# Log-sigmoid of the forget gates: one operand of each step in PSUM, the steps issued as one piece on VectorE

## The chip, the core and the metric

The kernel runs on one core of a Trainium2 chip. The metric is the device time of one execution in microseconds, from repeated runs; a profile is one further execution, taken by the hardware profiler. The work of the core is done by five engines that run at the same time, each with its own queue of instructions in a fixed order: TensorE (PE; its weight loads are PEld), VectorE (DVE), ScalarE (ACT), GpSimd (POOL) and SyncE (SP), which issues the transfers.

## What is computed

One layer of a streaming encoder on 512 tokens of 1024 channels, in float32: a half-step feed-forward block, then a mixing block, then a second half-step feed-forward block and a last RMS norm. In the mixing block one projection gives a convolution branch (512 channels, causal depthwise convolution of width 31, layer norm, swish) and an attention branch of 8 heads with 64 channels each. The attention has forget gates, which are what the change is about:

```
log_f = jax.nn.log_sigmoid(f_logit)               # (batch, 512, 8)
cum = jnp.cumsum(log_f, axis=1).transpose(0, 2, 1)
...
s = einsum("bqhd,bkhd->bhqk", qb, kb) * scale
s = s + cum[:, :, q0:q1, None] - cum[:, :, None, :q1]
s = where(kpos <= qpos, s, -inf)
p = softmax(s, axis=-1)
```

So no score of any head can be finished before the log-sigmoids of all tokens are there and summed up along the sequence.

## The kernel before, in words

**Products.** Channels lie on the 128 partitions and tokens along the free axis. Every large product is made in three passes of reduced precision: a weight tile of 128x1024 is loaded (raw), ScalarE makes its high part (whi), VectorE the low part (wlo, line 427), and TensorE multiplies whi with the high and the low part of the activations and wlo with the high part, eight groups of three matmuls of 512 columns for a tile (`product`, line 512). Three raw buffers and two of whi and wlo go round (line 60).

**Order of the mixing block** (line 51): the four convolution tiles c0 to c3, the values and gate logits (v), attention 0 and 1 (two heads each), the convolution branch's norm (n), attention 2 and 3, then the output projection. The convolutions 1 and 3 run on VectorE as 31 scalar_tensor_tensor steps each, with the accumulator in a PSUM bank (line 659); 0 and 2 run as a multiplication on ScalarE (tap) and an addition on GpSimd (acc, lines 664 and 665).

**Gates** (`values`, line 676). The product with the value and gate weights is spread over four banks; zf (128 tokens x 4 groups x 8 heads, so 32 numbers on each partition) is made from them by eight small VectorE steps (line 706). Then comes the log-sigmoid (lines 712 to 725): e1 = min(-z, z), e1 = exp(e1) on ScalarE, y = e1 / (e1 + 2), a series in y squared with nine terms, and lf = min(z, 0) - 2 times the series. All four tiles e1, e2, e3 and lf are in SBUF. For each half of the heads lf is copied to lfs (line 731), TensorE transposes it into a bank pc (line 735), a scan on VectorE gives the running sum (line 738), which goes to DRAM (cumd) and comes back spread over the partitions as ck (line 796) for the softmax of each head (lines 811 to 817). The transposed probabilities go through the bank of tag "pt", of which there is one (line 818).

**What sets the order.** All instructions are first recorded, then a planner in the kernel (`Plan.schedule`, line 245) puts them in an order for each engine, by prices of its own (`price`, line 221) and by ranks, the length of what hangs on an instruction plus an urgency (200 for the log-sigmoid, line 68). At each step it takes the instruction that can start first; of those that can start at the same moment, the one of highest rank. It counts 0.13 us from the end of a VectorE instruction to the start of one that reads its result (line 145), and 0.15 us to one on another engine. Between two `join` calls (line 172) all that is recorded is one unit: it is priced as the sum of its prices and nothing is put between its parts. The large products are kept in the order in which they are recorded (`in_turn`, line 507), a group of three matmuls being a unit; other work of TensorE is put between the groups. On the chip each engine runs its instructions in that fixed order, and waits where an input is late.

Of the kernel before, what the change touches and what calls it, by code (L numbers as in the profile page):

```python
# [24 lines left out]
F32 = mybir.dt.float32  # L25
F32R = mybir.dt.float32r
BF16 = mybir.dt.bfloat16
AF = mybir.ActivationFunctionType
ALU = mybir.AluOpType
AX = mybir.AxisListType  # L30

P = 128
# [9 lines left out]
H = 8  # L42
HD = 64
NT = T // P
# [15 lines left out]
LOADS, SPLITS, MISC, PT = 3, 2, 1, 1  # L60
# [280 lines left out]
def block_kernel(ctx: ExitStack, tc, x_d, w13a, w2a, wag, wvf, wqk, wo, w13b, w2b, par_d, out_d):  # L341
    nc = tc.nc
    plan = Plan(tc)
    V, S, PE = plan.engine("V", nc.vector), plan.engine("S", nc.scalar), plan.engine("PE", nc.tensor)
# [3 lines left out]
    pp = ctx.enter_context(tc.tile_pool(name="pp", bufs=1, space=bass.MemoryType.PSUM))  # L348
    dr = ctx.enter_context(tc.tile_pool(name="dr", bufs=1, space=bass.MemoryType.DRAM))

    def tile_(shape, tag, name, bufs=1, dt=F32):
        return plan.tile(sb, shape, dt, tag, name, bufs)

    def bank(tag, name, bufs=1):
        return plan.tile(pp, [P, T], F32, tag, name, bufs)

    def product_bank(name):
        return bank("mm", name, 3)

    def slot(n, name, dt=F32):  # L360

        return tile_([P, T], f"r{n}", name, 1, dt)
# [37 lines left out]
    for w13, w2 in ((w13a, w2a), (w13b, w2b)):  # L400
# [3 lines left out]
        if w13 is w13a:  # L404
            for piece in ORDER.split():
                n = int(piece[1:] or 0)
# [6 lines left out]
    def unit():  # L413
        i = taken[0]
        taken[0] += 1
        src, idx, k, c = units[i]
        raw = tile_([P, k, c], "raw", f"raw{i}", LOADS)
        hi = tile_([P, k, c], "whi", f"whi{i}", SPLITS, F32R)
        lo = tile_([P, k, c], "wlo", f"wlo{i}", SPLITS, F32R)
        load_and_split(i, raw, hi, lo, 0, k)  # L420
        return hi, lo
# [85 lines left out]
    def in_turn(step):  # L507

        for o in stream:
            step.before[id(o)] = o  # L510
# [162 lines left out]
    zf = tile_([P, NT, H], "zf", "zf")  # L673
    cum = []

    def values():
        plan.urgency = URGENT_V
        pr = bank("misc", "pr", MISC)
        PE.transpose(pr[:, :P], st.compact, ident)
        rcol = tile_([P, NT], "rcol", "rcol")  # L680
        V.tensor_copy(rcol, pr[:, 0:P:32])
        plan.urgency = 0.0
        for c in range(2):
            pv = [product_bank(f"pv{c}_{t}") if t < 2 else bank("s", f"pv{c}_{t}", 2) for t in range(NT)]
            for kh in range(2):
                hi, lo = unit()
                for t in range(NT):
                    ts_ = slice(t * P, (t + 1) * P)
                    o = pv[t][:, :VC]
                    head = None  # L690
                    for k in range(KD // 2):
                        kk = kh * (KD // 2) + k
                        step = plan.join("PE", head)
                        if head is None:
                            head = step
                            in_turn(step)
                        PE.matmul(o, xh[kk][:, ts_], hi[:, k], start=kk == 0, stop=False)
                        PE.matmul(o, xh[kk][:, ts_], lo[:, k], start=False, stop=False)
                        PE.matmul(o, xl[kk][:, ts_], hi[:, k], start=False, stop=kk == KD - 1)
                        plan.join(None)  # L700
                    stream[:] = [step]
            plan.urgency = URGENT_V
            for t in range(NT):
                rc = rcol[:, t:t + 1]
                S.activation(vt[:, t, 4 * HD * c:4 * HD * (c + 1)], pv[t][:, :4 * HD], AF.Copy, scale=rc)
                V.scalar_tensor_tensor(zf[:, t, 4 * c:4 * c + 4], pv[t][:, 4 * HD:VC], rc,
                                       par[:, G_FB + 4 * c:G_FB + 4 * c + 4], ALU.mult, ALU.add)
            plan.urgency = 0.0

        plan.urgency = URGENT_LF  # L710

        lf, e1, e2, e3 = (tile_([P, NT, H], n, n) for n in ("lf", "e1", "e2", "e3"))
        V.tensor_scalar(e1, zf, -1.0, None, ALU.mult)
        V.tensor_tensor(e1, e1, zf, ALU.min)
        S.activation(e1, e1, AF.Exp)
        V.tensor_scalar(e2, e1, 2.0, None, ALU.add)
        V.reciprocal(e2, e2)
        V.tensor_mul(e1, e1, e2)
        V.tensor_mul(e2, e1, e1)
        V.tensor_scalar(e3, e2, 1.0 / 17.0, None, ALU.mult)  # L720
        for n in (15, 13, 11, 9, 7, 5, 3):
            V.scalar_tensor_tensor(e3, e3, 1.0 / n, e2, ALU.add, ALU.mult)
        V.scalar_tensor_tensor(e3, e3, 1.0, e1, ALU.add, ALU.mult)
        V.tensor_scalar(e1, zf, 0.0, None, ALU.min)
        V.scalar_tensor_tensor(lf, e3, -2.0, e1, ALU.mult, ALU.add)


        for g in range(2):
            lfs = tile_([P, NT, P], "ew", f"lfs{g}", BUFS["ew"])
            G.memset(lfs, 0.0)  # L730
            V.tensor_copy(lfs[:, :, 0::32], lf[:, :, 4 * g:4 * g + 4])
            pc = bank("misc", f"pc{g}", MISC)
            plan.join("PE")
            for t in range(NT):
                PE.transpose(pc[:, t * P:(t + 1) * P], lfs[:, t], ident)
            plan.join(None)
            cs = slot((21, 14)[g], f"cum{g}")
            V.tensor_tensor_scan(cs, one, pc, 0.0, ALU.mult, ALU.add)

            rows = plan.tile(dr, [4, T], F32, f"cum{g}", f"cumd{g}")  # L740
            with plan.urgent(500.0):
                Q.dma_start(out=rows, in_=cs[0::32, :])
            cum.append(rows)

        plan.urgency = 0.0
# [134 lines left out]
    for piece in ORDER.split():  # L880
        n = int(piece[1:] or 0)
        if piece[0] == "c":
            conv_tile(n)
        elif piece[0] == "v":
            values()
        elif piece[0] == "a":
            attention(n)
        elif piece[0] == "n":
            plan.urgency = URGENT_LN
            rconv = conv_norm()  # L890
            plan.urgency = 0.0
        else:
            part = n // 2
            if n == 2:
                rattn = attn_stats.rstd()
            for j in range(2):
                w = unit()
                for d in (4 * (n % 2) + 2 * j, 4 * (n % 2) + 2 * j + 1):
                    w_out(part, d, w, rattn if part else rconv)
# [57 lines left out]
```

## Time and profile before

| | us |
|---|---|
| median of 3 runs | 980.85 |
| lowest, highest | 977.52, 983.25 |
| the profiled execution, its time | 982.02 |
| the profiled execution, its span (first to last instruction) | 979.0 |

Times inside the profile count from the start of the span. In a timeline a row gives the start, the duration, the engine, the line (a helper's line, L217, for all of them, so rows are told apart by the tiles), the operation, and out<-in with partitions x elements; behind it, in brackets, the idle time of that engine just before and what ended it. Buffer numbers are left out of the names: e is e1, e2 or e3, and conv the accumulator of convolution 3 in this stretch. A duration includes the time in which an instruction has started and is held up. [...]

### The profile page before, as it was taken

What the parts mean: (1) busy time and instruction counts of PE and PEld (TensorE: products, weight loads), DVE (VectorE), ACT (ScalarE), POOL (GpSimd) and SP (SyncE); (2) the same over time, 40 slices, a digit from 0 to 9 for tenths busy, and PEclk for the clock granted to TensorE, in tenths of its full rate; (3) what the DMA queues carried; (4) which work ended last, traced back from release to release, by engine and by line L of the source; (5) the groups of instructions that cost most, each with busy time, mean ns of one, the idle gap of its engine ahead of it and who ended that gap; (6) DMA issues with size and microseconds to landing.
All of it is one profiled execution on the core that took longest, in us unless ns stands there. A gap on an engine that the chain in (4) does not pass through costs nothing.

```text
span 979.0 us, 11641 instructions
## 1 busy us (share of the span) xinstructions
PE 953.4 (97%) x4687; PEld 777.2 (79%) x4687; DVE 518.5 (53%) x730; ACT 368.3 (38%) x528; POOL 109.8 (11%) x102
## 2 busy tenths in 40 slices
PE   8999999999999999996999999999999999999996
PEld 7888888888888888894666777888888888888885
DVE  6544442244444444989887867444443244444433
ACT  6423221123233325666558655332321122323230
POOL 2000000000000002899432100000000000000000
PEclk9999999999999999999898999999999999999998
DMA  7222332222233222221221212222332222223202
GB/s 242 85 90 104 105 116 88 79 93 101 88 114 118 89 86 74 88 93 71 71 71 34 87 51 80 95 99 89 113 118 90 85 86 89 105 93 132 90 30 87
DMA packets 26838, 91.07 MB, mean 93 GB/s; under 512 B 2840, under 2 KB 6040, under 8 KB 26784
## 3 DMA queue, kind: packets, MB, share of 16 engines
q1 hardware_dynamic: 26784, 90.33, 27.1%
q8 instruction: 36, 0.59, 0.2%
q14 instruction: 18, 0.15, 0.0%
HBM read 88.21 MB, written 2.11 MB: 92 GB/s over the span
## 4 chain that ended last, share of the span: by engine, by line
PE 86%; DVE 6%; ACT 2%; POOL 2%; DMA 1%; issue 1%; SPq 0%; DVEq 0%; POOLq 0%; ACTq 0%
PE f2o L217 12%; PE f2g L217 12%; PE f2u L217 12%; PE f1o L217 12%; PE f1u L217 12%; PE f1g L217 12%; PE wo L217 5%; DVE conv L217 2%; POOL acc L217 2%; PE pg L217 1%; PE pa L217 1%; PE po L217 1%; DVE e L217 1%; DMA x<-x_d 1%; PE s L217 1%
## 5 line engine op out<-in xcount | busy, mean ns | idle before, releaser
L217 ACT CAST whi<-raw 128x1024 fp32r<-128x1024 f32 (+3 forms) x153 | 165.9, 1085 | 476.8 <-issue 223.7
L217 DVE TENSOR_TENSOR wlo<-raw,whi 128x1024 fp32r<-128x1024 f32 (+3 forms) x153 | 198.2, 1296 | 30.8 <-ACT whi L217 29.1
L217 POOL TENSOR_TENSOR acc<-acc,tap 128x512 f32<-128x512 f32 x60 | 88.9, 1482 | 35.0 <-ACT tap L217 30.1
L217 PE MATMUL f2o<-f2ah,whi 128*128 128x512 f32 (+1 forms) x198 | 72.7, 367 | 0.0
L217 PE MATMUL f2o<-f2al,whi 128*128 128x512 f32 (+1 forms) x198 | 72.3, 365 | 0.0
L217 PE MATMUL f2o<-f2ah,wlo 128*128 128x512 f32 (+1 forms) x198 | 72.3, 365 | 0.0
L217 PE MATMUL f1u<-xh,whi 128*128 128x512 f32 x176 | 68.8, 391 | 0.6 <-ACT xh L217 0.6
L217 PE MATMUL f1u<-xl,whi 128*128 128x512 f32 x176 | 68.7, 390 | 0.3 <-DVE xl L217 0.3
L217 PE MATMUL f2g<-xh,whi 128*128 128x512 f32 x176 | 68.7, 390 | 0.0
L217 PE MATMUL f2u<-xh,whi 128*128 128x512 f32 x176 | 68.6, 390 | 0.0
L217 PE MATMUL f1u<-xh,wlo 128*128 128x512 f32 x176 | 68.5, 389 | 0.0
L217 PE MATMUL f2g<-xh,wlo 128*128 128x512 f32 x176 | 68.5, 389 | 0.0
L217 PE MATMUL f2u<-xh,wlo 128*128 128x512 f32 x176 | 68.5, 389 | 0.0
L217 PE MATMUL f2g<-xl,whi 128*128 128x512 f32 x176 | 68.5, 389 | 0.0
L217 PE MATMUL f1o<-f1ah,whi 128*128 128x512 f32 x176 | 68.5, 389 | 0.0
L217 PE MATMUL f1o<-f1al,whi 128*128 128x512 f32 x176 | 68.5, 389 | 0.0
L217 PE MATMUL f1o<-f1ah,wlo 128*128 128x512 f32 x176 | 68.5, 389 | 0.0
L217 PE MATMUL f2u<-xl,whi 128*128 128x512 f32 x176 | 68.5, 389 | 0.0
L217 PE MATMUL f1g<-xh,whi 128*128 128x512 f32 x168 | 65.5, 390 | 0.3 <-ACT whi L217 0.3
L217 PE MATMUL f1g<-xl,whi 128*128 128x512 f32 x168 | 65.5, 390 | 0.0
L217 PE MATMUL f1g<-xh,wlo 128*128 128x512 f32 x168 | 65.5, 390 | 0.0
L217 DVE TENSOR_TENSOR f2un<-f2u,rstd_f2in 128x512 f32<-128x512 f32 x22 | 15.2, 692 | 71.8 <-PE f2u L217 71.8
(231 smaller groups left out, 1768.1 us busy)
## 6 DMA issues: line engine op xcount, KB each, us to landing
raw<-w13b SPq DMA_DIRECT2D x44, 512.0 KB, 3.2
raw<-w13a SPq DMA_DIRECT2D x42, 512.0 KB, 3.3
raw<-w2a SPq DMA_DIRECT2D x16, 704.0 KB, 4.1
raw<-w2b SPq DMA_DIRECT2D x16, 704.0 KB, 4.0
raw<-wag SPq DMA_DIRECT2D x8, 512.0 KB, 3.2
raw<-wqk SPq DMA_DIRECT2D x8, 512.0 KB, 3.2
raw<-wo SPq DMA_DIRECT2D x8, 512.0 KB, 3.2
raw<-wvf SPq DMA_DIRECT2D x4, 520.0 KB, 3.1
```

The source lines that it names most:

```text
L217: ins = getattr(target, method)(*real, **kw)
```

## The change

The negation and the minimum become one instruction. One PSUM tile of tag "pt", with four slices p1 to p4, takes the exponential, the denominator (later min(z, 0)), y and y squared. Each later step reads at most one operand from SBUF and one from PSUM; the quotient is formed twice, once into PSUM (p3) and once into SBUF (e1), to multiply one by the other. The 16 VectorE steps after the exponential are recorded between `plan.join("V")` and `plan.join(None)`.

```diff
--- before.py
+++ after.py
@@ -707,22 +707,27 @@
                                        par[:, G_FB + 4 * c:G_FB + 4 * c + 4], ALU.mult, ALU.add)
             plan.urgency = 0.0
 
+
+
         plan.urgency = URGENT_LF
-
         lf, e1, e2, e3 = (tile_([P, NT, H], n, n) for n in ("lf", "e1", "e2", "e3"))
-        V.tensor_scalar(e1, zf, -1.0, None, ALU.mult)
-        V.tensor_tensor(e1, e1, zf, ALU.min)
-        S.activation(e1, e1, AF.Exp)
-        V.tensor_scalar(e2, e1, 2.0, None, ALU.add)
-        V.reciprocal(e2, e2)
-        V.tensor_mul(e1, e1, e2)
-        V.tensor_mul(e2, e1, e1)
-        V.tensor_scalar(e3, e2, 1.0 / 17.0, None, ALU.mult)
+        ps = plan.tile(pp, [P, 16, NT, H], F32, "pt", "e", PT)
+        p1, p2, p3, p4 = (ps[:, n] for n in range(4))
+        V.scalar_tensor_tensor(e1, zf, -1.0, zf, ALU.mult, ALU.min)
+        S.activation(p1, e1, AF.Exp)
+        plan.join("V")
+        V.tensor_scalar(p2, p1, 2.0, None, ALU.add)
+        V.reciprocal(e2, p2)
+        V.tensor_mul(p3, p1, e2)
+        V.tensor_mul(e1, p1, e2)
+        V.tensor_mul(p4, p3, e1)
+        V.tensor_scalar(e3, p4, 1.0 / 17.0, None, ALU.mult)
         for n in (15, 13, 11, 9, 7, 5, 3):
-            V.scalar_tensor_tensor(e3, e3, 1.0 / n, e2, ALU.add, ALU.mult)
-        V.scalar_tensor_tensor(e3, e3, 1.0, e1, ALU.add, ALU.mult)
-        V.tensor_scalar(e1, zf, 0.0, None, ALU.min)
-        V.scalar_tensor_tensor(lf, e3, -2.0, e1, ALU.mult, ALU.add)
+            V.scalar_tensor_tensor(e3, e3, 1.0 / n, p4, ALU.add, ALU.mult)
+        V.scalar_tensor_tensor(e3, e3, 1.0, p3, ALU.add, ALU.mult)
+        V.tensor_scalar(p2, zf, 0.0, None, ALU.min)
+        V.scalar_tensor_tensor(lf, e3, -2.0, p2, ALU.mult, ALU.add)
+        plan.join(None)
 
 
         for g in range(2):
```

## Rows read from the trace of the kernel before

**Rows 1.** Page, busy time and share of the span of each engine

```profile
PE 953.4 (97%) x4687; PEld 777.2 (79%) x4687; DVE 518.5 (53%) x730; ACT 368.3 (38%) x528; POOL 109.8 (11%) x102
```

**Rows 2.** Stretches: PE, PEld, DVE, ACT, POOL busy (instructions), PEclk, DMA

```profile
442.00:467.00 25.00, 15.59 (x68) 11.59 (x67) 24.91 (x39) 14.21 (x20) 21.45 (x16) 0.89 0.18 63
```

**Rows 3.** Timeline of TensorE, 444 to 467 us

```profile
444.84 0.50 PE L217 MATMUL pk<-xh,wlo 128*128 128x512 f32 x1 [0.70 <-DVE wlo L217]
...
445.89 0.40 PE L217 MATMUL pk<-xh,whi 128*128 128x512 f32 x1
...
451.35 0.50 PE L217 MATMUL pq<-xh,wlo 128*128 128x512 f32 x1 [0.73 <-DVE wlo L217]
...
457.36 0.46 PE L217 MATMUL s<-k,q 128*128 128x128 f32 x2 [0.73 <-DVE k L217]
...
460.51 0.50 PE L217 MATMUL pk<-xh,wlo 128*128 128x512 f32 x1 [1.78 <-DVE wlo L217]
466.46 1.12 PE L217 MATMUL pc<-ident,lfs 128*128 128x128 f32 x4 [5.46 <-DVE lfs L217]
```

**Rows 4.** Timeline of VectorE in the chain's stretch, 442 to 467 us

```profile
442.27 0.17 DVE L217 TENSOR_SCALAR e<-zf 128x32 f32<-128x32 f32 x1
...
443.06 0.59 DVE L217 TENSOR_TENSOR e<-e,zf 128x32 f32<-128x32 f32 x1
443.57 1.21 DVE L217 TENSOR_TENSOR wlo<-raw,whi 128x1024 fp32r<-128x1024 f32 x1
...
455.93 0.68 DVE L217 SCALAR_TENSOR_TENSOR e<-e,e 128x32 f32<-128x32 f32 x1
...
457.13 0.83 DVE L217 SCALAR_TENSOR_TENSOR e<-e,e 128x32 f32<-128x32 f32 x1
...
466.24 0.24 DVE L217 COPY lfs<-lf 128x16 f32<-128x16 f32 x2
```

**Rows 5.** Instructions that read or write the chain's tiles e1 to e3

```profile
L217 DVE SCALAR_TENSOR_TENSOR e<-e,e x8: 614/786/1269, 451.2 to 462.2; 128x32 f32<-128x32 f32 x8
...
L217 DVE RECIPROCAL e<-e x1: 340/340/340, 446.6 to 446.6; 128x32 f32<-128x32 f32 x1
L217 DVE TENSOR_TENSOR e<-e,e x1: 173/173/173, 447.4 to 447.4; 128x32 f32<-128x32 f32 x1
```

**Rows 6.** Timeline of GpSimd, two additions of convolution 2

```profile
455.27 1.30 POOL L217 TENSOR_TENSOR acc<-acc,tap 128x512 f32<-128x512 f32 x1
...
456.64 1.27 POOL L217 TENSOR_TENSOR acc<-acc,tap 128x512 f32<-128x512 f32 x1
```

**Rows 7.** Groups of VectorE instructions in 380 to 560 us

```profile
L217 DVE SCALAR_TENSOR_TENSOR conv<-u,par,conv 128x512 f32<-128x512 f32 x60 | 44.8, 747 | 0.7
```

**Rows 8.** Instructions that write the gate logits zf (duration min/median/max)

```profile
L217 DVE SCALAR_TENSOR_TENSOR zf<-pv,rcol,par x8: 206/216/224, 425.5 to 441.5; 128x4 f32<-128x4 f32 x8
```

**Rows 9.** Timeline of VectorE, an instruction and one that reads its result

```profile
553.09 0.68 DVE L217 TENSOR_TENSOR t<-wo,rstd_conv 128x512 f32<-128x512 f32 x1
553.81 0.69 DVE L217 TENSOR_TENSOR x<-x,t 128x512 f32<-128x512 f32 x1
```

**Rows 10.** Timeline of ScalarE, the chain's exponential

```profile
443.68 0.23 ACT L217 ACTIVATE e<-e 128x32 f32<-128x32 f32 x1 [0.22 <-DVE e L217]
```

**Rows 11.** Busy time in stretches of 5 us, the columns of rows 2

```profile
465.00:470.00 5.00, 3.54 (x11) 2.96 (x12) 4.97 (x8) 0.00 (x0) 0.61 (x1) 0.50 0.01 2
...
490.00:495.00 5.00, 3.22 (x24) 2.24 (x22) 5.00 (x5) 2.82 (x6) 4.13 (x3) 1.00 0.53 170
495.00:500.00 5.00, 4.79 (x24) 3.30 (x25) 4.23 (x16) 2.07 (x7) 0.00 (x0) 0.66 0.01 3
...
530.00:535.00 5.00, 3.10 (x15) 1.73 (x16) 3.57 (x8) 4.99 (x8) 2.94 (x3) 0.80 0.01 3
```

**Rows 12.** Timeline of VectorE, softmax scaling steps of attention 0

```profile
492.12 2.83 DVE L217 TENSOR_SCALAR sm<-sm,st 128x512 f32<-128x512 f32 x2
...
510.48 0.48 DVE L217 TENSOR_SCALAR sm<-sm,st 128x512 f32<-128x512 f32 x1
```

## The prediction

> **What bounds the kernel now.** I read the page first. TensorE is busy for 97% of the span and VectorE for about half [rows 1], so a faster VectorE chain is worth only what TensorE waits for it. Next I read the table of stretches, to find where TensorE is not busy: in 442 to 467 us it is busy for 15.59 of 25 us while VectorE is busy for 24.91 [rows 2]. There, and for these 25 us only, VectorE is the bound. The timeline of TensorE names the waits one by one [rows 3]: 0.70 us and 0.73 us for a low part of a weight (wlo), 0.73 us for k, 1.78 us for the next wlo, and 5.46 us for lfs, the product of the log-sigmoid chain: 9.40 us together. TensorE runs its instructions in order, so while the transposes of lfs wait, the rest of the key product of attention 1 waits behind them.
>
> Then I read VectorE in the same stretch [rows 4]. The chain starts at 442.27 and its result is copied to lfs at 466.24, 24.0 us for 17 small steps on 32 columns and one exponential. Two things make it long. First, the planner puts one other instruction (a convolution tap, a wlo, a piece of q or k) between any two steps. Second, a step itself takes a median of 786 ns in the eight-fold form, while the same size took 173 ns once [rows 5]. What is the difference? The step that starts at 455.93 ends at 456.61 and the one at 457.13 ends at 457.96 [rows 4]; GpSimd's additions of the other convolution end at 456.57 and 457.91 [rows 6]. Steps end when a GpSimd instruction ends. So most of a step is a wait for GpSimd, and the chain goes at GpSimd's pace, one step for each addition, about 1.37 us. The convolution taps in between take SBUF u and a PSUM accumulator, and the mean of sixty is 747 ns for 512 columns [rows 7]: they don't show that wait.
>
> [...]
>
> **The change part by part.** Removed: the separate -z and minimum become one instruction, and the steps after the exponential each read one operand from PSUM. Added: one multiplication more (the quotient is formed twice), so the piece has 16 instructions where 15 stood. Moved: the piece is one unit to the planner. No DMA is added; the loads of cumd and ck move up on SP's queue with the chain, past weight loads that are issued well ahead, at no cost. The PSUM bank is the one of tag "pt", whose first other use is attention 0's transposes, which follow from cum and so cannot come earlier: cost nothing.
>
> What a step costs now is in no row, since no row has 32 columns with PSUM. Bounds: below, the uncontended step of 173 ns [rows 5]; above, the 747 ns of a tap that also reads and writes PSUM [rows 7]. The nearest is zf, 216 ns for 4 columns with a PSUM input [rows 8]. From 4 to 512 columns the time goes from 216 to 747 ns, 1.05 ns a column, so 32 columns give 0.245 us. A dependent step starts a little after the end of the one before: 553.81 after 553.09 + 0.68, 0.04 us [rows 9]. So 15 steps of 0.28 us and a reciprocal of 0.34 + 0.07 us [rows 5] are 4.6 us; by the lower bound it is 16 x 0.21 = 3.4 us, by the upper 16 x 0.79 = 12.6 us. I take 4.6, as zf is of the same kind and size.
>
> [...]
>
> Start of the piece: the first step at 442.27 (0.17), a tap, then wlo, which stood behind the second step at 443.57 and can now start at 443.06; it takes 1.2 [rows 4], to 444.3. The exponential ran at 443.68 [rows 10], and now needs only the first step. By the planner's prices (lines 221 to 243) a tap then goes first, as it is ready a hair sooner. So the piece runs from about 444.9 to 449.5, another tap goes in before the copy (0.7), and the copy, with both sides in SBUF, may wait half of one GpSimd addition: lfs at 450.9.
>
> What waits behind the piece on VectorE? The wlo and q of the next products, by 4.6 us at most; the wlo is wanted by TensorE at 451 (0.73 late before), but TensorE is standing at lfs by then.
>
> Where does TensorE stand? This is the term that decides. The planner orders TensorE by its own prices. Before, it counted 15 steps of 0.10 with one 0.66 tap each, 12.7 with two wlo in place of taps; the piece is priced 6 x 0.095 + 0.265 + 9 x 0.098 = 1.71, plus one tap. So in its own clock (which gives an order here and no time) the chain ends 10.4 sooner, and it moves the transposes up by 15 groups of three matmuls (0.65 each) and two s products: from behind the first group of the second pk to behind the second group of the first pk. TensorE gets there early: its third pk matmul started at 444.84, the seventh at 445.89 [rows 3], both now about 0.5 earlier, 445.4. It waits from 445.4 to 450.9, **5.5 us**: the wait for lfs is not removed, it moves forward. The planner's 1.71 for a piece that takes 4.6 is the reason.
>
> The sum: waits before 9.40; after 5.5 for lfs and 0.2 for the first wlo. The second wlo, the k and the third wlo (0.73, 0.73, 1.78) have VectorE 5 to 6 us less loaded and come in time. Gain 9.40 - 5.7 = 3.7. [...] The profiled execution took 982.02 (span 979.0 and 3.0 around it): 978.3 by this gain. It stands 1.2 above the median of the three runs, 980.85, so the forecast is **977.1**. By the piece's lower bound (1.2 sooner) it is 975.9; with a step of 0.4 us it is 979.
>
> **Rivals.** *More comes back* (0.22). Attention 0 starts some 10 us sooner, and VectorE has slack. TensorE idles 1.78 us in 490 to 495 behind softmax steps and is at 0.66 of its clock in 495 to 500, another 1.7 us [rows 11]. If both go: 977.1 - 3.5 = 973.6; with the piece at its lower bound too, 972.4. For it: VectorE was full there. Against: GpSimd still adds then.
>
> *Given back* (0.12). In 530 to 535 TensorE is busy 3.10 of 5 us and ScalarE 4.99 [rows 11]: the output projection waits for the convolution branch's norm. If that chain doesn't move up, TensorE waits the 3.7 there: 980.9. Against: that chain follows TensorE's own sums.
>
> *The step's price stays* (0.07). If GpSimd is not the cause, or writing PSUM is dear, 16 steps of 0.79 without pause put lfs at 458.4+, waits are 13.2 against 9.4: 984.7. It decides from 0.52 us a step. The change would then shorten nothing.
>
> *Attention 0 meets GpSimd* (0.14), the slower side. Its eight scale-by-1/sum steps, SBUF to SBUF, are moved up among the taps of GpSimd. Two of 512 columns took 2.83 us among taps, one 0.48 when GpSimd was idle [rows 12]: 0.94 lost each, 7.5 for eight. 1.8 of that is in the wait of 490 to 495 already. If the planner's new order makes TensorE stand for the rest, with half speed after two such waits: 977.1 + 5.7 + 3.4 = 986.2. It is slower than before from 3.7 us of such waits on. Against: before, most of them already ran among taps.
>
> **How the numbers follow.** The forecast has 0.45, with a range of its own of 974.5 to 979.5. About 0.5%, 4.9 us, is what a measurement of this kernel can tell. Faster by more (below 975.9): all of the first rival and some 0.4 of the forecast, 0.40. Slower by more (above 985.8): two thirds of the last rival and some of the third, 0.13. The rest 0.47. The range leaves out the tail of the first rival and the last one: 970 to 984.5.
>
> **What would show it.** Right: steps of 0.2 to 0.3 us in one block, about 4.6 us, near 445; lfs near 451; TensorE's wait for lfs of 4 to 6 us inside the first pk, with half clock behind it; no waits for wlo and k over 0.3 us up to 470; 467 to 560 nearly as before. Wrong: steps over 0.5 us; a wait for lfs under 3 us; or TensorE waits on softmax over 4 us before 500.

## The result, and the profile after

The changed kernel takes **969.14 us** (median of 6 runs, 968.43 to 970.01) and the kernel before took 979.06 us beside it (6 runs, 975.9 to 983.25). The ratio is 0.9892 [0.9874, 0.9910]: 9.9 us or 1.1% faster. The forecast of 977.1 had the sign right and the size too small, and the time lies below the range. A later pair on another occasion gave 969.3 and 978.34.

First the page of the changed kernel, the line that answers to [rows 1]. TensorE's busy time falls by 4.1 us although it computes the same: part of the gain is not a shorter wait but a faster clock (a mean of 0.992 in its profiled execution, 0.985 in that of before).

```profile
PE 949.3 (98%) x4687; PEld 774.7 (80%) x4687; DVE 511.9 (53%) x730; ACT 368.3 (38%) x528; POOL 109.8 (11%) x102
```

Next the stretches, with the columns of [rows 2] and [rows 11]; PEclk is the clock granted to TensorE, as a share of its full speed.

```profile
442.00:467.00 25.00, 20.79 (x90) 16.28 (x89) 22.84 (x53) 14.46 (x27) 18.27 (x13) 0.86 0.31 94
...
445.00:450.00 5.00, 0.97 (x6) 0.84 (x5) 4.52 (x20) 3.73 (x5) 4.69 (x5) 0.66 0.28 97
450.00:455.00 5.00, 5.00 (x19) 4.04 (x18) 3.87 (x4) 0.72 (x1) 3.85 (x3) 0.66 0.31 107
...
490.00:495.00 5.00, 4.93 (x28) 2.60 (x27) 4.88 (x14) 2.07 (x7) 1.91 (x1) 1.00 0.30 105
495.00:500.00 5.00, 5.00 (x25) 4.04 (x25) 4.87 (x13) 4.17 (x9) 0.52 (x1) 1.00 0.32 105
...
520.00:525.00 5.00, 3.49 (x21) 1.80 (x20) 4.87 (x10) 4.99 (x8) 2.96 (x3) 1.00 0.02 3
525.00:530.00 5.00, 4.39 (x41) 2.08 (x39) 4.97 (x7) 4.95 (x9) 2.67 (x4) 1.00 0.01 2
530.00:535.00 5.00, 5.00 (x40) 3.95 (x32) 3.16 (x11) 4.61 (x10) 0.00 (x0) 1.00 0.66 207
```

In the chain's own stretch TensorE is busy for 20.79 us where it was for 15.59 [rows 2]. It still stands idle in 445 to 450 and runs at a granted clock of 0.66 there and in the five us behind. In 490 to 500 it no longer stands, and the clock that was 0.66 in 495 to 500 [rows 11] is 1.00. The stretches from 520 on matter as much: TensorE idles 2.1 us between 520 and 530, about as much as it idled before in this part of the kernel, and yet the clock stays at 1.00. The kernel before, in the same view, had this behind its idle time of 530 to 535 [rows 11]:

```profile
535.00:540.00 5.00, 5.00 (x25) 2.40 (x28) 3.66 (x6) 4.12 (x7) 2.70 (x4) 0.52 0.06 15
```

That is nearly five us at half the full clock (0.52), which the prediction had not read. These are TensorE's waits near 495 and 530 in the kernel before:

```profile
495.21 1.02 PE L217 MATMUL s<-k,q 128*128 128x256 f32 x2 [1.99 <-DVE st L217]
...
530.25 0.30 PE L217 MATMUL pt<-ident,sm 128*128 128x128 f32 x1 [0.36 <-DVE sm L217]
531.20 0.73 PE L217 MATMUL s<-k,q 128*128 128x512 f32 x2 [0.66 <-DVE st L217]
...
532.56 0.42 PE L217 MATMUL ssq_conv<-sq_conv,ones 128*32 128x128 f32 x8 [0.55 <-POOL sq_conv L217]
...
534.11 0.79 PE L217 MATMUL wo<-yl,whi 128*128 128x512 f32 x1 [0.44 <-DVE yl L217]
```

Now TensorE's timeline in the changed kernel. Its waits answer to those of [rows 3].

```profile
443.93 0.50 PE L217 MATMUL pk<-xh,wlo 128*128 128x512 f32 x1 [0.18 <-DVE wlo L217]
...
444.73 0.40 PE L217 MATMUL pk<-xh,wlo 128*128 128x512 f32 x1
449.16 1.11 PE L217 MATMUL pc<-ident,lfs 128*128 128x128 f32 x4 [4.03 <-DVE lfs L217]
...
521.54 0.74 PE L217 MATMUL s<-k,q 128*128 128x512 f32 x2 [1.16 <-DVE st L217]
...
524.08 0.50 PE L217 MATMUL wo<-yl,whi 128*128 128x512 f32 x1 [0.35 <-DVE yl L217]
...
526.08 0.44 PE L217 MATMUL pt<-ident,sm 128*128 128x128 f32 x2 [0.22 <-ACT pT L217]
...
527.71 0.50 PE L217 MATMUL wo<-yl,whi 128*128 128x512 f32 x1 [0.38 <-DVE yl L217]
```

The four waits for wlo, wlo, k and wlo [rows 3] are down to one of 0.18 us. The wait for lfs is still there, 4.03 us where it was 5.46, and it has moved forward by 17 us into the first pk. VectorE's timeline of the changed kernel shows why it is so long:

```profile
441.87 0.19 DVE L217 SCALAR_TENSOR_TENSOR e<-zf 128x32 f32<-128x32 f32 x1
...
444.45 0.19 DVE L217 TENSOR_SCALAR e<-e 128x32 f32<-128x32 f32 x1
...
445.99 1.74 DVE L217 SCALAR_TENSOR_TENSOR e<-e,e 128x32 f32<-128x32 f32 x8
...
447.99 0.19 DVE L217 SCALAR_TENSOR_TENSOR lf<-e,e 128x32 f32<-128x32 f32 x1
448.10 0.75 DVE L217 SCALAR_TENSOR_TENSOR conv<-u,par,conv 128x512 f32<-128x512 f32 x1
448.76 0.42 DVE L217 COPY lfs<-lf 128x16 f32<-128x16 f32 x2
```

The piece is one block, its steps starting 0.2 to 0.4 us apart, from 444.45 to 448.18, 3.73 us, beside GpSimd at work for 4.69 of the 5 us. The eight-fold step has this row among the instructions on the tiles e (against [rows 5]):

```profile
L217 DVE SCALAR_TENSOR_TENSOR e<-e,e x8: 186/187/189, 446.0 to 447.5; 128x32 f32<-128x32 f32 x8
```

Where did the time come from? I added up TensorE's idle time in stretches of 1 us, and what its busy time lost to the clock (busy time times one minus the granted clock), from 440 to 560 us. In us, idle / lost to the clock:

| profiled execution | span | 440–480 | 480–515 | 515–560 | span less all of it |
|---|---|---|---|---|---|
| before | 979.0 | 9.43 / 2.55 | 2.10 / 1.65 | 2.02 / 3.19 | 958.1 |
| after | 967.1 | 4.62 / 2.14 | 0.07 / 0 | 2.11 / 0 | 958.2 |

The remainder is the same, so these terms add up to the whole difference of 11.9 us between the spans: 6.7 us of idle time (4.8 in the chain's stretch, 2.0 near 495) and 5.2 us of clock (0.4, 1.65 and 3.2). The medians differ by 9.9 only, since the profiled execution of before (982.02) lies 3 us above the median of its runs.

### The profile page after: what moved, and what is told of

Its sections match the earlier page's. It is cut to its first block, busy times and chain, and to the rows that moved or that the text cites. A ratio compares the mean times of both kernels' runs of the same rounds, so it can differ in the third digit from the quotient of the medians.

```text
span 967.1 us, 11642 instructions
## 1 busy us (share of the span) xinstructions
PE 949.3 (98%) x4687; PEld 774.7 (80%) x4687; DVE 511.9 (53%) x730; ACT 368.3 (38%) x528; POOL 109.8 (11%) x102
## 3 DMA queue, kind: packets, MB, share of 16 engines
HBM read 88.21 MB, written 2.11 MB: 93 GB/s over the span
## 4 chain that ended last, share of the span: by engine, by line
PE 89%; DVE 4%; POOL 3%; ACT 2%; issue 1%; DMA 0%; SPq 0%; DVEq 0%; POOLq 0%; ACTq 0%
PE f2o L217 13%; PE f2g L217 12%; PE f2u L217 12%; PE f1o L217 12%; PE f1g L217 12%; PE f1u L217 12%; PE wo L217 5%; POOL acc L217 3%; PE pk L217 2%; PE pq L217 1%; PE pg L217 1%; PE pa L217 1%; PE po L217 1%; PE s L217 1%; DVE conv L217 1%
```

## The experiments

My theory after the result: the PSUM operands free the steps of GpSimd, the planner's low price for the piece leaves the wait for lfs, and the rest of the gain is the clock near 500 and 535. The rivals: that joining alone is enough; that the gain near 495 and 535 comes from the order only; and that the clock falls independently of the waits.

**The PSUM operands without the joined piece.**

```diff
-        plan.join("V")
...
-        plan.join(None)
```

> The changed kernel without the join: the steps keep their PSUM operand but are recorded one by one, so other VectorE work may stand between them. Lock theory (a step with SBUF operands waits for GpSimd): steps of about 0.19 us with one tap of 0.66 between them, lfs near 457 us, no wait of TensorE for lfs over 1 us, as TensorE gets to the transposes only near 458; 966 to 970 us if the removed waits are all that counts. Order theory (the gain comes from the piece being together): steps of 0.6 to 0.8 us as before, lfs near 465, 979 us. Attention theory (the later gain comes from attention 0 starting earlier): waits gone but half clock at 495 to 500 and 530 to 540 stays, 972 to 975 us.

It took 971.22 us, ratio 0.9913 [0.9883, 0.9944]. Three rows of VectorE's timeline, then the first transposes of lfs on TensorE's, both of this kernel:

```profile
452.58 0.18 DVE L217 SCALAR_TENSOR_TENSOR e<-e,e 128x32 f32<-128x32 f32 x1
452.68 0.75 DVE L217 SCALAR_TENSOR_TENSOR conv<-u,par,conv 128x512 f32<-128x512 f32 x1
453.33 0.18 DVE L217 SCALAR_TENSOR_TENSOR e<-e,e 128x32 f32<-128x32 f32 x1
```

```profile
457.23 0.72 PE L217 MATMUL pc<-ident,lfs 128*128 128x128 f32 x4 [2.09 <-DVE lfs L217]
```

A step takes 0.18 us and the chain still goes, for the most part, at one step for each other instruction, but with a tap between them the next step now starts 0.75 us later (452.58 to 453.33) instead of about 1.37. The wait for lfs is 2.09, shorter than in the changed kernel, because the planner left the transposes late. So the operands alone give 7.6 of the 9.9 us (the two intervals overlap). The lock theory holds for the steps and for lfs near 457, but it missed the wait (under 1 us) and the time (up to 970). In the terms of the table this kernel has 3.77 / 1.67, 0.08 / 0 and 3.35 / 3.04 us: the stretch of 480 to 515 is free as in the changed kernel, but the half clock behind 520 stays, as the attention theory had it for that place. The operands alone do not remove it.

**The joined piece without the PSUM operands**, in the kernel before:

```diff
+        plan.join("V")
         V.tensor_scalar(e2, e1, 2.0, None, ALU.add)
...
         V.scalar_tensor_tensor(lf, e3, -2.0, e1, ALU.mult, ALU.add)
+        plan.join(None)
```

> The kernel before with the steps after the exponential joined into one piece, all operands in SBUF. Lock theory: each of the 15 steps still waits for a GpSimd addition, about 1.3 us each, the piece takes 15 to 20 us, TensorE waits 15 to 20 us for lfs, 985 to 992 us. Order theory: with nothing in between the steps are 0.2 us, the piece takes 4 us, 969 us.

979.04 us, ratio 0.9992 [0.9975, 1.0008]: joining alone is worth nothing. The steps on the tiles e, and TensorE's wait, in this kernel:

```profile
L217 DVE SCALAR_TENSOR_TENSOR e<-e,e x8: 193/665/1302, 448.9 to 454.5; 128x32 f32<-128x32 f32 x8
```

```profile
455.89 1.11 PE L217 MATMUL pc<-ident,lfs 128*128 128x128 f32 x4 [9.72 <-DVE lfs L217]
```

The piece takes 9.6 us (445.50 to 455.08), less than the 15 to 20 that I expected, and the time is below the 985 to 992 that went with it: only seven additions ran beside the 15 steps, and some steps follow another at 0.19 us without meeting one. The 9.72 us at one place took the place of most of the five waits, and the idle time of 440 to 480 even grew (11.97 against 9.43). The wait near 495 is gone here too (0 / 0), which wins that back, and 515 to 560 stays as before (1.80 / 3.22).

**Is it GpSimd?** The same kernel without GpSimd's additions of convolution 2:

```diff
-                G.tensor_add(a, a, t)
+                if i != 2:
+                    G.tensor_add(a, a, t)
```

> The joined piece with all operands in SBUF, as in the run join_only, with the 30 additions of convolution 2 on GpSimd left out, so that convolution 2 is the first tap only. Lock theory: with GpSimd idle the SBUF steps take about 0.19 us each, as the PSUM steps do, and the piece about 3.6 us instead of 9.6, with lfs near 449. Rival (SBUF operands or the piece itself are slow): steps of 0.6 to 1.1 us stay and the piece takes 9 us or more.

One execution, of 969.21 us; it leaves out a part of the layer, so only the steps are compared. A row of the tiles e:

```profile
L217 DVE SCALAR_TENSOR_TENSOR e<-e,e x8: 191/192/194, 446.2 to 447.8; 128x32 f32<-128x32 f32 x8
```

With both inputs in SBUF and GpSimd's additions gone, a step is 192 ns and the piece 3.5 us (444.94 to 448.42). Nothing of the instructions themselves was slow: the 665 ns are GpSimd's doing. That is shown.

**The planner's price for the piece.** It priced the piece at 1.71 where it takes 3.73. Two prices of my own: the number is added to the planner's, so that the piece counts 3.7, about what it takes, and then 6.2, more than it takes:

```diff
-        plan.join("V")
+        plan.join("V").cost = 2.0
```

> The changed kernel with 2.0 us added to the planner's price of the piece, which then is 3.7, what the piece takes on the chip. The transposes move behind the sixth group of the first pk. Theory that the wait for lfs is the planner's under-pricing: the wait falls from 4.0 to 1 to 1.5 us, the half clock behind it goes or shortens, 964 to 967 us. Rival (what is won there is given back later, since another order follows): the wait falls and the time stays at 968 to 970.

```diff
-        plan.join("V")
+        plan.join("V").cost = 4.5
```

> The changed kernel with 4.5 us added to the planner's price of the piece. The transposes move behind the first group of the second pq, attention 0 starts some 5 us later than in the changed kernel in the planner's order. Theory of the under-pricing: no wait for lfs, no half clock near 450, 963 to 966 us. Attention theory: the later start brings the half clock at 495 to 540 back, 967 to 972 us.

The first took 976.05 us (0.9966 [0.9946, 0.9987]), the second 969.41 (0.9893 [0.9861, 0.9926]). With 2.0, VectorE and TensorE show:

```profile
448.91 2.09 DVE L217 TENSOR_TENSOR wlo<-raw,whi 128x1024 fp32r<-128x1024 f32 x1
450.93 1.31 DVE L217 COPY lfs<-lf 128x16 f32<-128x16 f32 x2
```

```profile
452.22 1.12 PE L217 MATMUL pc<-ident,lfs 128*128 128x128 f32 x4 [3.51 <-DVE lfs L217]
...
528.70 0.65 PE L217 MATMUL ssq_conv<-sq_conv,ones 128*32 128x128 f32 x8 [4.00 <-POOL sq_conv L217]
```

Both expectations are missed. The wait hardly fell (3.51, where I expected 1 to 1.5), as a wlo went ahead of the two copies to lfs, which are SBUF to SBUF and took 1.31 us beside GpSimd's additions instead of 0.42 (0.25 in the kernel without the additions). A new order also put a wait of 4.00 us before the sums of the convolution branch. A small change of price moved the time by 7 us, most of it far from the chain. With 4.5, TensorE shows:

```profile
451.37 0.66 PE L217 MATMUL pc<-ident,lfs 128*128 128x128 f32 x4 [0.67 <-DVE lfs L217]
...
519.68 0.30 PE L217 MATMUL pt<-ident,sm 128*128 128x128 f32 x1 [0.81 <-DVE sm L217]
...
520.65 0.43 PE L217 MATMUL ssq_conv<-sq_conv,ones 128*32 128x128 f32 x8 [0.67 <-POOL sq_conv L217]
...
522.20 0.80 PE L217 MATMUL wo<-yl,whi 128*128 128x512 f32 x1 [0.70 <-DVE yl L217]
```

Here the wait for lfs is as good as gone and the clock does not fall behind it: 3.47 / 0 in 440 to 480 against 4.62 / 2.14, which is 3.3 us better. Of these only 1.15 are idle time, as other waits come in, 0.62 us for a wlo and 1.02 for q among them. So the price decides where this wait lies and how long it is, but the price that is right for the piece, 2.0 more, did not remove it. The time is that of the changed kernel: three waits of 0.81, 0.67 and 0.70 us within 3 us are followed by half clock, which costs 3.27 us in 515 to 560. In the profiled execution the gain is given back there. The four runs of this kernel fall into two groups, 967.7 and 968.5 us at a mean clock of 0.995, and 970.3 and 970.9 at 0.992.

**The copies inside the piece**, to take the tap and the wlo from between the chain and lfs:

```diff
+        lfss = [tile_([P, NT, P], "ew", f"lfs{g}", BUFS["ew"]) for g in range(2)]
+        for lfs in lfss:
+            G.memset(lfs, 0.0)
         plan.join("V")
...
+        for g in range(2):
+            V.tensor_copy(lfss[g][:, :, 0::32], lf[:, :, 4 * g:4 * g + 4])
         plan.join(None)
...
-            lfs = tile_([P, NT, P], "ew", f"lfs{g}", BUFS["ew"])
-            G.memset(lfs, 0.0)
-            V.tensor_copy(lfs[:, :, 0::32], lf[:, :, 4 * g:4 * g + 4])
+            lfs = lfss[g]
```

> The changed kernel with the two copies of lf to lfs in the piece, so that no tap stands between. The copy comes 0.7 us earlier, and the planner puts the transposes one group (0.68 us) earlier too, behind the first group of the first pk. Theory that the planner's under-pricing sets the wait: the wait for lfs stays at 4.0 us (3.7 to 4.3) and the time within 968 to 970.5. Rival: the wait falls by the 0.7 us, 968 us or less.

And with a price:

```diff
-        plan.join("V")
+        plan.join("V").cost = 3.0
```

> The copies in the piece and 3.0 us added to the planner's price. In the run price2_0 the copies stood behind a wlo of 2.1 us and took 1.3, so the wait stayed at 3.5; here nothing stands between. The transposes come behind the sixth group of the first pk, near 447.5, lfs near 448.7: a wait of 1.0 to 1.8 us, and no half clock near 450. The time is 965 to 968 if the output projection is not later than in the changed kernel; if the planner's later order of the convolution norm counts (as in price2_0, with a wait of 4.0 for its sums), 971 to 975.

They took 971.64 us (0.9921 [0.9897, 0.9945]) and 972.14 us (0.9912 [0.9883, 0.9941]). The first is a miss on both sides: the transposes moved forward as well, the two copies took 0.88 us instead of 0.42, so that lfs came no earlier (449.3), and the wait grew to 4.7 us. In the second the wait for lfs is 1.4 us, with no half clock near 450 (0 us lost to it in 440 to 480), as expected, but TensorE then shows, ahead of the output projection, a wait for a softmax result:

```profile
524.35 0.69 PE L217 MATMUL pt<-ident,sm 128*128 128x128 f32 x2 [4.22 <-DVE sm L217]
```

Its 515 to 560 hold 4.80 / 2.65 us where the changed kernel's hold 2.11 / 0. What is won near 450 is lost near 525 again.

**Does the clock follow the waits?** Useless sums are put where TensorE waits, in the kernel with the price of 4.5. The first try repeats each sum of the convolution branch with zero weights:

```diff
+    zeros = tile_([P, 32], "zeros", "zeros")
+    G.memset(zeros, 0.0)
...
-                for g in range(NT):
-                    PE.matmul(self.ps[32 * g:32 * (g + 1), :w], (ones if weight is None else weight)[:, :32],
-                              piece[:, g * w:(g + 1) * w], start=len(self.parts) == 1, stop=last)
+                again = 2 if self.name == "conv" else 0
+                for r in range(again + 1):
+                    for g in range(NT):
+                        real = r == (0 if len(self.parts) == 1 else again)
+                        PE.matmul(self.ps[32 * g:32 * (g + 1), :w],
+                                  (zeros if not real else ones if weight is None else weight)[:, :32],
+                                  piece[:, g * w:(g + 1) * w], start=real and len(self.parts) == 1,
+                                  stop=real and last)
```

> The run price4_5 with two sets of four matmuls by zero weights added to each of the four sums of the convolution branch's norm, 2.9 us of TensorE work that changes no value, put where TensorE waits before the output projection. Clock theory (the half clock near 520 to 530 follows from those packed waits, and costs 3.3 us): with the gaps partly filled the half clock goes in most runs, the granted clock is 0.995, and the time is 967 to 969.5 in spite of the added work. Rival (the clock there doesn't hang on these gaps): the half clock stays and the time is 970.5 to 973.

985.98 us, ratio 1.0063 [1.0042, 1.0083]: slower by 17 us, far more than such matmuls cost (40 records of them take 1.30 us in the row of (2) below). The test said nothing on the clock; something else was in it. The next three kernels take it apart: the tile of zeros alone (1), the first sum done five times with no new tile (2), and the price of 4.5 once more (3).

```diff
+    zeros = tile_([P, 32], "zeros", "zeros")
+    G.memset(zeros, 0.0)
```

> The run price4_5 with the tile of 32 zeros of price4_5_fill made and set, but no sums added: only the addresses of all tiles allocated after it move. Address theory (price4_5_fill lost its time because every matmul of the kernel ran 2% slower at full clock, 217 instead of 222 matmuls in 50 us, with the tiles moved): 980 to 984 us, the same slow spacing in the first feed-forward block. Rival (the added sums cost it): 968 to 971 us.

```diff
-                for g in range(NT):
-                    PE.matmul(self.ps[32 * g:32 * (g + 1), :w], (ones if weight is None else weight)[:, :32],
-                              piece[:, g * w:(g + 1) * w], start=len(self.parts) == 1, stop=last)
+                for again in reversed(range(5 if self.name == "conv" and len(self.parts) == 1 else 1)):
+                    for g in range(NT):
+                        PE.matmul(self.ps[32 * g:32 * (g + 1), :w],
+                                  (ones if weight is None else weight)[:, :32],
+                                  piece[:, g * w:(g + 1) * w], start=len(self.parts) == 1,
+                                  stop=last or again > 0)
```

> The run price4_5 with the first of the four sums of the convolution norm done five times over (16 matmuls of 128 columns more, about 1.4 us), in the gaps before the output projection; no tile is added. Clock theory: the granted clock is 0.995 in most runs and the time 967 to 969. Rival: the clock is at 0.992 in half of the runs or more, as in price4_5, and the time 969.5 to 972.

```diff
-        plan.join("V")
+        plan.join("V").cost = 4.5
```

> The run price4_5 unchanged, on the same chip as the others of this call. Between 967.5 and 971, in two groups by the granted clock (0.992 and 0.995), as in the first run.

(1) 985.49 us, ratio 1.0067 [1.0043, 1.0091]; (2) 967.59 us, 0.988 [0.9852, 0.9908]; (3) 968.59 us, 0.9893 [0.9867, 0.9919]. So it was the tile, of which the last section tells; (1) lies even above the 980 to 984 expected of it. For the clock, (2) was meant to be read against (3). TensorE's timeline in (2):

```profile
522.26 0.30 PE L217 MATMUL pt<-ident,sm 128*128 128x128 f32 x1 [0.81 <-DVE sm L217]
...
523.24 1.30 PE L217 MATMUL ssq_conv<-sq_conv,ones 128*32 128x128 f32 x40 [0.68 <-POOL sq_conv L217]
524.47 0.50 PE L217 MATMUL wo<-yh,whi 128*128 128x512 f32 x1
```

The stretches of (2), and those of (3):

```profile
520.00:525.00 5.00, 3.52 (x50) 2.43 (x49) 4.35 (x9) 4.99 (x7) 2.26 (x3) 1.00 0.01 3
525.00:530.00 5.00, 4.89 (x43) 2.57 (x42) 4.87 (x9) 4.97 (x10) 3.78 (x4) 1.00 0.00 1
```

```profile
520.00:525.00 5.00, 3.63 (x22) 1.82 (x22) 4.21 (x7) 5.00 (x9) 3.90 (x4) 0.68 0.01 3
525.00:530.00 5.00, 5.00 (x31) 2.53 (x31) 3.63 (x7) 3.60 (x6) 1.48 (x3) 0.63 0.02 9
```

The first two waits (0.81, 0.68) are in (2) as in the price of 4.5; the third (0.70) is filled with matmuls that compute nothing new, and the clock stays at 1.00: 515 to 560 lose 0 us to it, against 3.20 in (3). Taken alone, that would say that filling the wait kept the clock. But (1), where nothing is filled, shows this:

```profile
529.37 0.30 PE L217 MATMUL pt<-ident,sm 128*128 128x128 f32 x1 [0.78 <-DVE sm L217]
530.34 0.43 PE L217 MATMUL ssq_conv<-sq_conv,ones 128*32 128x128 f32 x8 [0.67 <-POOL sq_conv L217]
...
531.88 0.50 PE L217 MATMUL wo<-yl,whi 128*128 128x512 f32 x1 [0.70 <-DVE yl L217]
```

```profile
525.00:530.00 5.00, 3.89 (x18) 2.59 (x17) 4.42 (x12) 4.96 (x9) 0.76 (x1) 1.00 0.00 0
530.00:535.00 5.00, 3.97 (x35) 2.11 (x35) 4.41 (x6) 4.98 (x9) 4.35 (x5) 1.00 0.01 3
```

They are the same three waits, and 515 to 560 lose 0 us to the clock here too, though in a kernel whose matmuls follow one another some 2% more slowly. Besides, the profiled execution of (3) is the only one of its four runs with a mean clock of 0.992; the other three have 0.995 or 0.996, those of (2) 0.994 to 0.997. So the runs do not show that the useless sums kept the clock, and the third rival is not ruled out: the fall may simply have been absent from the execution of (2) that was profiled. In the medians (2) is 1.0 us below (3), and in its profiled execution it lost 3.3 us ahead of 440. 967.59 is the lowest median of the study, but its runs (966.62 to 969.4) overlap with those of the changed kernel (968.43 to 970.01), so I don't call it a better version. Of (3), 966.95 to 970.03, one run lies just below what was expected.

**The changed kernel once more**, without an edit, beside the last three:

> The changed kernel, on the same chip as the others of this call: 968 to 970.5. If the planner's price is worth something beyond it, price4_5 with the clock held is below by 1 to 2 us; if what is won at the transposes is given back later, none of them is below.

969.3 us, ratio 0.9901 [0.9877, 0.9924], which is 1.7 us above (2), and 4.66 / 2.27, 0.06 / 0 and 2.12 / 0 us in the three stretches: the account of the first section holds in a second profiled execution.

## Why the prediction was right in its mechanism and wrong in its size

**GpSimd as the cause of the long steps: right.** 665 ns with its additions and 192 without, on the same operands and in the same joined order. With one operand in PSUM a step takes 187 ns while GpSimd is busy for 4.69 of 5 us (445 to 450 in the changed kernel).

**The step's duration: mis-sized.** The sum took 0.28 us a step from zf and an interval of 0.04, so 4.6 us for the piece. A step is 0.187 us, steps start 0.22 apart, and the piece takes 3.73: near the lower bound of 3.4. The row zf was a poor neighbour: its 216 ns carry something that is not the PSUM input, as the steps of 187 ns have one too. The eight-fold step is no longer with its PSUM operand: 187 ns against 192 with two in SBUF and GpSimd's additions gone.

**The wait that stays: right, its size off in part by the same term.** It lies where the prediction put it, behind the second group of the first pk, with a tap between the piece and the copies and half clock behind it (0.50 in 449 to 453). It lasts 4.03 us instead of 5.5: the piece is 0.9 us shorter than in the sum, and it also started 0.45 sooner. The gain in 440 to 480 is 4.8 instead of 3.7. That the planner's price sets the wait, the stated reason, is borne out by the price of 4.5, with which 0.67 us of it is left; the price that fits the piece (2.0 added) left 3.51.

**The step that failed: the sum ends at 467, and "467 to 560 nearly as before".** The forecast's gain of 3.7 us is made of the waits in 442 to 467 alone. The sum counts nothing for the clock behind the wait for lfs. That was the author's estimate; the two profiled executions show 2.55 us lost in 440 to 480 before and 2.14 after. But the stretches behind were put at nothing too, and there 2.0 us of idle time near 495 and 4.8 us lost to the clock (1.65 near 500, 3.2 near 535) are gone, 6.8 of the 11.9 us between the profiled executions. The prediction saw the first two as a rival, "More comes back", at 0.22, priced at 3.5 (measured 2.0 + 1.65). It did not see the last at all: it read 530 to 535 (0.80) as the output projection's wait for the convolution branch's norm, which might grow, and not the next five us at 0.52. By the rows above, about half of that wait is for softmax results (0.36 and 0.66). The waits in this place add up to about as much as before (2.0 and 2.1 us). Only their spread is different: before, there were 0.36, 0.66, 0.55 and 0.44 within 4 us, now 1.16, 0.35, 0.22 and 0.38 over 6 us. That this spread is why the clock now stays is not shown: (1) keeps 1.00 behind 0.78, 0.67 and 0.70 us, and the kernel with the copies in the piece behind 0.40, 0.66 and 0.69 within 4 us. What the runs show is that the half clock there is gone in both profiled executions of the changed kernel, and still there with the operands alone (3.04) and with joining alone (3.22).

**What stays open.** Why the half clock near 535 is gone is open, as just said. The wait near 495 (1.99 us for a softmax sum) is gone or at most 0.7 us in every variant, also with joining alone, where VectorE's steps stay slow (a median of 665 ns), and with PSUM alone, where TensorE's order is late. Whether VectorE's smaller backlog or the earlier start of attention 0 removes it, the runs don't tell apart. The changed kernel's first 440 us are 1.0 us less idle than before's (1.90 against 2.93), which varies between 1.6 and 3.9 over all kernels; in the table's remainder it is hidden by more busy time elsewhere. How much of the 4.8 us of clock is in the medians is open too: there is one trace of the kernel before, at a mean clock of 0.985, and its runs go from 0.983 to 0.991. The 14 runs at 0.990 and 0.991 average 976.9 us, which is 7.8 above the changed kernel instead of 9.9.

**The rivals.** *The step's price stays* is out (187 ns). *Given back* did not happen with the change. What it describes, a wait for the convolution branch's norm ahead of the output projection, came with the price of 2.0 (4.00 us). The copies at 3.0 lost their gain to a wait for softmax (4.22), the price of 4.5 to the clock. *Attention 0 meets GpSimd* did not show: 490 to 500 holds 0.07 us of idle time.

## What to carry to other kernels

When a small VectorE step takes several times its own duration while GpSimd is at work, as here (a median of 786 ns, where the same size took 173 once), try one operand in PSUM before anything else: here that brought the steps to 0.18 us and gave 7.6 us, and joining the steps without it gave nothing. When a long wait of TensorE is taken out or moved, price the clock of every later group of waits too, by reading the granted clock of the stretches behind them: 4.8 of the 11.9 us between the two profiled executions were there. And when a planner orders the work by prices, a piece that is priced at half its duration can leave a wait ahead of its result; check a new price by the whole span, since the order far behind it changes as well.

## What the runs showed of the hardware that was not expected

**A small tile shifts everything.** A tile of 128 bytes in each partition, made near the start and never read, made the kernel 16.9 us slower (985.49 against 968.59), at full clock and in stretches that it has nothing to do with. The stretch 100 to 150 us in the kernel with the price of 4.5, then in the one with the added tile:

```profile
100.00:150.00 50.00, 50.00 (x222) 41.44 (x221) 20.55 (x22) 13.20 (x14) 0.00 (x0) 1.00 0.36 122
```

```profile
100.00:150.00 50.00, 50.00 (x217) 40.35 (x216) 22.18 (x25) 13.77 (x15) 0.00 (x0) 1.00 0.32 108
```

In both TensorE is busy all the time at a clock of 1.00, with 222 matmuls in one and 217 in the other: from one to the next it takes 2.3% longer. That the tile moves the addresses of the tiles made after it, and that this is the reason, is the author's inference: no trace here shows an address, and no run tried another size. An experiment that adds a tile needs a run with the tile alone beside it.

**The time follows the mean clock, run by run.** Over 45 runs of the kernel before, those with a mean clock of 0.985 took 980.9 us on average (17 runs) and those with 0.991 took 976.7 (6 runs). The changed kernel's first six runs show no such order (0.992 to 0.996, 968.43 to 970.01). A single profiled execution is one draw of that, and a gain that consists of clock should be read from many.
